# New prices for single operations in the planner of a hybrid decoder layer

## The chip, the cores and the metric

The kernel is one program on one core of a Trainium2 chip. Its time is device microseconds (us) of that core, from the program's start to its end; several runs are taken and the median is given. The engines are named as the profile names them: PE is the matrix engine TensorE (PEld its loads of weights), DVE is VectorE, ACT is ScalarE, POOL is GpSimd, SP is SyncE, which issues nearly all loads.

## The reference

One decoder layer for 512 tokens of width 2048, all in float32:

```python
mod_all = silu(c) @ w_ada + b_ada                    # 6 vectors of 2048
h = rms_norm(x, norm1_g) * (1 + sc1) + sh1
u = h @ w_in                                         # conv | q | 3 x (k, v) | gates
y_conv = B * causal_depthwise_conv3(C * H)
y_attn = g0 * compressed + g1 * selected + g2 * window   # 8 heads x 128, 2 kv heads
x = x + g1 * ([rms_norm(y_conv) | rms_norm(y_attn)] @ w_out)
h = rms_norm(x, norm2_g) * (1 + sc2) + sh2
x = x + g2 * (relu(h @ w_ff1) ** 2 @ w_ff2)          # inner width 8192
out = rms_norm(x, normf_g)
```

## The kernel before

**How the work is tiled.** Tokens lie along the free dimension, 512 of them or two halves of 256; the 2048 channels are 16 blocks of 128 partitions. Every large product is made of three matmuls, high x high, high x low and low x high: each operand is split into a high part (a copy on ACT into the type fp32r) and a low part (a subtraction on DVE, `x - high`). So a block of weights of 128 x 1024 (512 KB) comes by a load of SP, costs ACT one copy and DVE one subtraction, and feeds 24 matmuls of TensorE. The two large products of the feed-forward part are made by seven block products instead of eight (B1, U6, T5, B2, T7, B3, T4 in the code, by sums of the four blocks of weights on DVE and of the tokens); the results of some of the seven are combined out of PSUM on DVE, and the chains "a", "b" and "c" (table `CHAIN`) say which of the seven add onto one PSUM bank. T4 adds onto the bank of T7 after T7's sum has been read from it.

**What runs in which order.** Three programs follow each other, each with a planner of its own:

1. The opening, the modulation vectors, the projections and the convolution (line 369, 16 passes). `mod_all` is made on DVE: 190 *dots* (`dot`, line 470) multiply 1024 weights by silu(c) on each of 128 partitions and sum them into one column; each takes a load of 512 KB into one of eight tiles wa. Meanwhile TensorE works through the key, value, convolution, gate and query columns. `rope` (line 659) rotates keys and queries with two *half rotations*, products on 64 partitions each.
2. Attention (line 1066, 6 passes), eight blocks of 128 queries and one kv head: scores s, a maximum, Exp on ACT, `cf = gate / sum` on DVE (a reciprocal and a product on 128 x 4), transposes on TensorE into pt, a split of these into tt (ACT, then DVE), and products pv. Between them stand the columns of `out_conv`, 16 blocks of 24 matmuls with weights from mix.
3. The rest of the output projection, the feed-forward part and the last norm (line 1233, one pass). The first product's results, squared, are split into gt (three tiles in turn, line 1259) and gb (one tile, line 1260) by `outcome` (line 1444) and stored to device memory g by GpSimd, 256 KB at a time; the second product loads them back. Weights of this part are split into a ring of three tiles hl (line 1240) and, for the first of the plan, tiles sg and gt.

**The planner.** Class `Order` stands between the code and the engines. `record` keeps each operation as a node with what it must follow: data, a tile's earlier readers, and the slots of the one ring of 29 tiles "m". `price` (line 126) gives each node a cost, the time for which it holds its engine, and a lag, after which another engine may use its result; on one engine, DVE or TensorE, the next operation may follow as soon as the cost is over. `plan` simulates the engines: it computes for each node the latest time at which it may begin (`late`, from the times at which TensorE wants its matmuls) and then takes, again and again, the node that can begin first, and among those the one with the earliest `late`. A load or store ends some time after a model of the wire (lines 308 and 309): 1.5 us from its issue at the least, its size at 340 GB/s (410 in the first 40 us), and 0.7 us (2.8 in the first 40 us). Stores into g count 1.3 times their size. With several passes the matmuls' planned times of one pass are the wanted times of the next, and in every second the planned order of the matmuls is kept; the pass with the shortest total wins (line 223). With one pass the matmuls stay in the order of the code, apart from a few marked as floating, among them those that sum squares and spread a norm's factor over the partitions.

`emit` (line 212) then issues all operations sorted by their planned begin (line 237). Each engine takes its own in that order, whatever happens: an operation that waits holds back all that stand behind it on its engine. The planned times themselves reach the chip in no other way.

Of the kernel before, what the change touches and what calls it, by code (L numbers as in the profile page):

```python
# [16 lines left out]
P = 128  # L17
# [40 lines left out]
class Order:  # L58
# [67 lines left out]
    def price(self, eng, op, out, ins, kw):  # L126

        n = Order.width(out)
        if "dma" in op:
            return (0.42 if eng == "sync" else 0.55), 0.0  # L130
        if eng == "tensor":
            if op == "matmul" and ins[0].name.startswith("ones"):
                return n * 0.0017, 0.2
            if op == "matmul" and ins[0].dtype == F32:
                return max(self.wide[0], n * self.wide[1]) * out.shape[0] / P, 0.2
            return (0.109 if op == "transpose" else max(0.1, n * self.pace)), 0.2
        if eng == "scalar":
            aps = len(ins) - 1
            more = 0.1 if kw.get("accum_out") is not None else 0.0
            return (0.18 if n < 16 else 0.09 + 0.00084 * n + (0.09 * max(0, aps) if not more else 0.19)), 0.16  # L140
        if eng == "gpsimd":
            return 0.15 + 0.0024 * n, 0.3
        if op == "tensor_reduce":
            rows = max(Order.width(x) for x in ins)
            return 0.18 + 0.00104 * rows * (1.75 if n > 16 else 1), 0.14
        if n < 16:
            return (0.2 if op == "reciprocal" else 0.14), 0.14
        if op == "scalar_tensor_tensor":
            return 0.14 + 0.00101 * n + (0.087 if kw.get("accum_out") is not None else 0.0), 0.14
        if op in ("tensor_scalar", "tensor_copy", "memset") and all(  # L150
                x.space != bass.MemoryType.PSUM for x in [out] + ins):
            return 0.13 + 0.0005 * n, 0.14
        strided = any(abs(list(x.ap)[-1][0]) > 1 for x in [out] + ins)
        return 0.068 + n * (0.00185 if strided else 0.00104) + (0.1 if out.shape[0] < P else 0.0), 0.14

    def record(self, eng, op, real, args, kw):
        is_ap = lambda x: hasattr(x, "dep_tracking_offset")
# [90 lines left out]
    def plan(self, ideal, t, fixed):  # L248
        nodes = self.nodes
        ends = {}  # L250
        for name, by in self.seen.items():
            for i in set(by):
                ends.setdefault(i, []).append(name)
        users = {name: len(set(v)) for name, v in self.seen.items()}
        mine = sorted((n for x in nodes for n in x.born), key=lambda n: int(n.rsplit("_", 1)[1]))
        rank = {n: k for k, n in enumerate(mine)}

        for x in reversed(nodes):
            move = x.cost + x.lag if not x.size else 2.5 + x.size / Order.RATE
            x.late = min([nodes[s].late - (move if nodes[s].eng != x.eng or x.eng not in ("tensor", "vector") else x.cost)  # L260
                          for s in x.succs] + [ideal.get(x.i, t + 10.0 - x.due)])

        free = dict.fromkeys(("tensor", "vector", "scalar", "sync", "gpsimd"), 0.0)
        wire = 0.0
        ready = {e: [] for e in free}
        lanes = {}
        for i in fixed or [x.i for x in nodes if x.eng == "tensor" and not x.loose]:
            lanes.setdefault(0 if fixed else nodes[i].lane, []).append(i)
        for lane in lanes.values():
            lane.reverse()  # L270
        slots = sorted([0.0] * (self.count - len(self.outer)))
        given = []
        while slots and len(given) < len(mine):
            given.append(slots.pop(0))
        for x in nodes:
            x.left, x.ready = len(x.preds), 0.0
            if not x.left and (x.eng != "tensor" or x.loose):
                ready[x.eng].append(x)
        out = []
        while len(out) < len(nodes):  # L280
            best = None
            for e in free:
                c = [(x, 0, None) for x in ready[e]]
                if e == "tensor":
                    c = [(x, -1, None) for x in ready[e]]
                    c += [(nodes[q[-1]], k, q) for k, q in lanes.items() if q and not nodes[q[-1]].left]
                for x, k, q in c:
                    at = max(free[e], x.ready + x.slack, wire - 2.0 if x.size else 0.0)
                    if x.born:
                        last = max(rank[n] for n in x.born)  # L290
                        if last >= len(given):
                            continue
                        at = max(at, given[last])
                    key = (at, k, x.late, x.i)
                    if best is None or key < best[0]:
                        best = key, x, q
            (at, *_), x, q = best
            e = x.eng
            if q is not None:
                q.pop()  # L300
            else:
                ready[e].remove(x)
            x.begin = at
            free[e] = at + x.cost
            end = at + x.cost + x.lag
            if x.size:
                wire = max(wire, at + 1.5)
                wire += x.size / (Order.RUSH if wire < self.rush else Order.RATE)
                end = wire + (2.8 if wire < self.rush else 0.7)
            for n in ends.get(x.i, ()):  # L310
                users[n] -= 1
                if not users[n] and (n in rank or n in self.outer) and n not in self.kept:
                    if len(given) < len(mine):
                        given.append(max([end] + given[-1:]))
            for s in x.succs:
                y = nodes[s]
                y.left -= 1
                y.ready = max(y.ready, free[e] if e == y.eng and e in ("tensor", "vector") else end)
                if not y.left and (y.eng != "tensor" or y.loose):
                    ready[y.eng].append(y)  # L320
            out.append(x)
        return max(free.values()), out
# [1497 lines left out]
```

## Time and profile before

| what | us |
|---|---|
| median of 3 runs | 2052.33 |
| lowest and highest | 2050.72 and 2052.61 |
| the profiled execution | 2051.98 |
| its span, first to last instruction | 2050.2 |
| granted TensorE clock over the span | 0.998 of full speed |

The profile is of one execution. What lies around its span (1.78 us) is the start and end of the program. Busy times overlap between engines, and TensorE's busy time is a model of pipelined matmuls, so it is to be read together with the number of matmuls in a stretch. The profile's lines all name line 162, since `record` issues everything; instructions are told apart by their tiles: "pf<-tk,hl" writes tile pf and reads tk and hl. An idle time stands in brackets with what ended it.

### The profile page before, as it was taken

The numbers are of one execution on the slowest core, as the hardware profiler recorded it, in microseconds if no ns is written. First come the engines' busy times: TensorE is split into PE (matmuls) and PEld (weight loads), VectorE is DVE, ScalarE is ACT, GpSimd is POOL, SyncE is SP. The second block draws the span as 40 slices with busy tenths as digits, with TensorE's granted clock in tenths as the row PEclk, the third lists the DMA queues.
The fourth block names the chain that finished last, engine by engine and source line by source line (L and its number), as shares of the span: only waits on it lengthen the run. The fifth ranks groups of instructions, "written<-read, shape, count | busy, mean of one in ns | idle before, by whom it ended". The sixth has DMA issues, their size and how long they took to land. (4 is left out here: it accounts for less than half of the span.)

```text
span 2050.2 us, 38160 instructions
## 1 busy us (share of the span) xinstructions
PE 2039.0 (99%) x15038; PEld 1905.5 (93%) x15038; DVE 1854.6 (90%) x3007; ACT 1031.0 (50%) x1564; POOL 128.2 (6%) x244
## 2 busy tenths in 40 slices
PE   9999999999999999999999999999999999999998
PEld 7888778898888789999999999999999999999998
DVE  8999768898898657999999999999999999999998
ACT  7664222323556436766666666666433333333355
POOL 0000000000000001122121121211000000000000
PEclk9999999999999999999999999999999999999999
DMA  9996789997221253567767767679876466466452
GB/s 388 341 344 215 285 311 342 339 334 256 77 97 34 92 205 116 179 211 216 216 197 212 210 201 215 202 207 333 301 272 240 144 242 240 145 234 243 152 171 104
DMA packets 142676, 454.25 MB, mean 222 GB/s; under 512 B 15776, under 2 KB 18208, under 8 KB 142496
## 3 DMA queue, kind: packets, MB, share of 16 engines
q1 hardware_dynamic: 108448, 387.83, 54.7%
q0 software_dynamic: 34048, 63.98, 10.3%
q8 instruction: 118, 1.93, 0.4%
q14 instruction: 62, 0.51, 0.1%
HBM read 383.59 MB, written 68.16 MB: 220 GB/s over the span
## 5 line engine op out<-in xcount | busy, mean ns | idle before, releaser
L162 PE MATMUL pf<-tk,hl 128*128 128x256 f32 x10704 | 1218.9, 276 | 2.3 <-ACT hl L162 1.1
L162 PEld LDWEIGHTS pf<-tk,hl 128*128 128x128 f32 x10704 | 1217.2, 188 | 2.8 <-ACT hl L162 1.3
L162 ACT ACTIVATE hl<-rw 128x1024 fp32r<-128x1024 f32 x269 | 285.6, 1062 | 323.7 <-PE pf L162 276.1
L162 DVE TENSOR_TENSOR hl<-rw,hl 128x1024 fp32r<-128x1024 f32 (+2 forms) x351 | 335.9, 967 | 28.6 <-ACT hl L162 27.7
L162 ACT ACTIVATE hl<-sg 128x1024 fp32r<-128x1024 f32 x180 | 191.0, 1062 | 230.6 <-PE pf L162 186.1
L162 DVE SCALAR_TENSOR_TENSOR t<-wa,cs 128x1024 bf16<-128x1024 f32 x190 | 232.0, 1221 | 28.5 <-DMA wa<-in_w_ada 25.2
L162 PE MATMUL ps<-h_m,wh 128*128 128x512 f32 x1080 | 248.8, 389 | 0.0
L162 PEld LDWEIGHTS ps<-h_m,wh 128*128 128x128 f32 x1080 | 202.5, 188 | 43.1 <-issue 1.2
L162 ACT ACTIVATE wh<-raw 128x1024 fp32r<-128x1024 f32 (+1 forms) x105 | 112.0, 1067 | 248.1 <-PE ps L162 207.5
L162 DVE TENSOR_TENSOR hl<-sg,hl 128x1024 fp32r<-128x1024 f32 (+2 forms) x193 | 187.8, 984 | 23.9 <-ACT hl L162 23.8
L162 PE MATMUL ps<-h,wh 128*128 128x512 f32 x840 | 195.8, 390 | 0.7 <-DVE h L162 0.5
L162 PEld LDWEIGHTS ps<-h,wh 128*128 128x128 f32 x840 | 157.0, 188 | 35.4 <-issue 1.2
L162 DVE TENSOR_TENSOR wh<-raw,wh 128x1024 fp32r<-128x1024 f32 (+1 forms) x106 | 129.9, 1225 | 27.3 <-ACT wh L162 26.7
L162 DVE TENSOR_TENSOR sg<-sg,rw 128x1024 f32<-128x1024 f32 x120 | 146.7, 1222 | 3.0
L162 DVE SCALAR_TENSOR_TENSOR x<-pf,mod,x 128x256 f32<-128x256 f32 (+1 forms) x280 | 128.8, 484 | 13.7 <-PE pf L162 12.2
L162 POOL DMA_DIRECT2D g<-gt x192 | 101.2, 532 | 382.1 <-DVE gt L162 217.9
L162 PE MATMUL pw<-mix,wh 128*128 128x512 f32 x384 | 108.6, 404 | 0.0
L162 ACT ACTIVATE t<-t 128x512 f32<-128x512 f32 (+2 forms) x130 | 74.0, 572 | 11.8 <-DVE t L162 9.9
L162 PEld LDWEIGHTS pw<-mix,wh 128*128 128x128 f32 x384 | 68.5, 189 | 10.6
L162 DVE TENSOR_TENSOR sg<-rw 128x1024 f32<-128x1024 f32 x60 | 73.0, 1217 | 5.7 <-DMA rw<-in_w_f 5.5
L162 DVE TENSOR_TENSOR rw<-rw 128x1024 f32<-128x1024 f32 x60 | 72.9, 1215 | 0.0
L162 DVE TENSOR_TENSOR gt<-t,gt 128x512 fp32r<-128x512 f32 x96 | 65.5, 683 | 0.5 <-ACT gt L162 0.5
(222 smaller groups left out, 1708.8 us busy)
## 6 DMA issues: line engine op xcount, KB each, us to landing
rw<-in_w_f SPq DMA_DIRECT2D x263, 512.0 KB, 4.2
wa<-in_w_ada SPq DMA_DIRECT2D x192, 512.0 KB, 6.4
tk<-g SPq DMA_DIRECT2D x114, 512.0 KB, 6.5
g<-gt POOLq DMA_DIRECT2D x192, 256.0 KB, 5.0
raw<-in_w_conv SPq DMA_DIRECT2D x32, 512.0 KB, 4.6
x<-in_xt SPq DMA_DIRECT2D x16, 512.0 KB, 5.5
raw<-in_w_kv SPq DMA_DIRECT2D x16, 512.0 KB, 5.1
raw<-in_w_cv SPq DMA_DIRECT2D x16, 512.0 KB, 4.5
```

Of the source, the lines that this page charges most:

```text
L162: x.i, x.eng, x.call = len(self.nodes), eng, (lambda: real(*args, **kw))
```

## The change

Prices of single operations in `price`, and the planned end of a store by GpSimd in `plan`. No operation is added or removed, and none changes its operands; the planner is run with the new prices.

```diff
         if eng == "scalar":
-            aps = len(ins) - 1
-            more = 0.1 if kw.get("accum_out") is not None else 0.0
-            return (0.18 if n < 16 else 0.09 + 0.00084 * n + (0.09 * max(0, aps) if not more else 0.19)), 0.16
+            if n < 16:
+                return 0.09 * len(ins), 0.16
+            base = (0.045 if ins[0].space == bass.MemoryType.PSUM else 0.09) + 0.00084 * n
+            return base + (0.09 * (len(ins) - 1) if kw.get("accum_out") is None else 0.19), 0.16
...
         if op == "tensor_reduce":
             rows = max(Order.width(x) for x in ins)
-            return 0.18 + 0.00104 * rows * (1.75 if n > 16 else 1), 0.14
+            return 0.06 + 0.00104 * rows * (1.75 if n > 16 else 1), 0.14
         if n < 16:
-            return (0.2 if op == "reciprocal" else 0.14), 0.14
+            return (0.09 if op == "reciprocal" else 0.14 if op == "scalar_tensor_tensor" else 0.075), 0.14
         if op == "scalar_tensor_tensor":
-            return 0.14 + 0.00101 * n + (0.087 if kw.get("accum_out") is not None else 0.0), 0.14
+            given = hasattr(kw["scalar"], "dep_tracking_offset")
+            return (0.14 + 0.00101 * n if given else 0.08 + 0.00103 * n), 0.14
+        if op == "memset":
+            return 0.01 + 0.00075 * n, 0.14
+        if op == "tensor_scalar" and ins[0].space == bass.MemoryType.PSUM:
+            return 0.135 + 0.00104 * n, 0.14
...
         strided = any(abs(list(x.ap)[-1][0]) > 1 for x in [out] + ins)
-        return 0.068 + n * (0.00185 if strided else 0.00104) + (0.1 if out.shape[0] < P else 0.0), 0.14
+        return 0.068 + n * (0.0017 if strided else 0.00104), 0.14
...
                 wire += x.size / (Order.RUSH if wire < self.rush else Order.RATE)
-                end = wire + (2.8 if wire < self.rush else 0.7)
+                end = wire + (2.8 if wire < self.rush else 2.3 if e == "gpsimd" else 0.7)
```

`n` is the number of elements of the output on one partition, `ins` are the operands that lie in memory (so a scale or bias that is a column counts as one), and `given` is true where the scalar of the operation is a column of values, false where it is a number.

| operation | price before | price after |
|---|---|---|
| dot, 1024 | 1.261 | 1.135 |
| half rotation, 512 | 0.700 | 0.600 |
| ACT copy out of PSUM, 512 | 0.520 | 0.475 |
| reciprocal on 128 x 4 | 0.200 | 0.090 |
| product on 128 x 4 | 0.140 | 0.075 |
| a store of 256 KB into g, issue to end | 3.2 | 4.8 |

## The prediction

> **What bounds the kernel now.** I read the page first, then the busy time by stage, then who makes TensorE wait, then the timeline at those waits. The page:
>
> ```profile
> span 2050.2 us, 38160 instructions
> ## 1 busy us (share of the span) xinstructions
> PE 2039.0 (99%) x15038; PEld 1905.5 (93%) x15038; DVE 1854.6 (90%) x3007; ACT 1031.0 (50%) x1564; POOL 128.2 (6%) x244
> ```
>
> The reader is to see that TensorE has 11.2 us of idle time in all (2050.2 - 2039.0), and that VectorE is the next fullest engine. The busy time by stage follows; the columns are the stretch, its length, then busy time and (instructions) of PE, PEld, DVE, ACT and POOL, the granted clock, DMA share and GB/s:
>
> ```profile
> 25.00:200.00 175.00, 174.52 (x770) 144.12 (x769) 168.76 (x252) 105.62 (x192) 0.00 (x0) 1.00 0.85 320
> 200.00:500.00 300.00, 300.00 (x1570) 251.71 (x1569) 249.50 (x383) 81.52 (x109) 0.00 (x0) 1.00 0.88 318
> 500.00:700.00 200.00, 200.00 (x1040) 162.99 (x1039) 164.92 (x455) 112.89 (x269) 0.00 (x0) 1.00 0.24 80
> 700.00:775.00 75.00, 75.00 (x417) 65.67 (x416) 42.60 (x56) 28.77 (x40) 3.65 (x6) 1.00 0.46 157
> 775.00:950.00 175.00, 173.37 (x1507) 173.03 (x1506) 164.04 (x303) 120.88 (x209) 26.28 (x48) 1.00 0.59 181
> 950.00:1400.00 450.00, 450.00 (x3969) 450.00 (x3968) 428.91 (x592) 286.01 (x402) 87.94 (x167) 1.00 0.69 208
> 1400.00:1990.00 590.00, 590.00 (x5197) 590.00 (x5196) 567.85 (x847) 245.86 (x257) 10.15 (x20) 1.00 0.66 229
> 1990.00:2050.00 60.00, 52.80 (x460) 52.07 (x459) 51.16 (x101) 34.69 (x70) 0.00 (x0) 0.97 0.28 97
> ```
>
> A busy TensorE could still hide slow matmuls, so I divide: 450.00 us by 3969 is 113.4 ns a matmul, and 590.00 by 5197 is 113.5. Two long stages at one pace, at a granted clock of 1.00, mean that nothing holds TensorE there. Idle time stands in three rows only: 0.48 us in the first, 1.63 in the fifth (175.00 - 173.37), 7.20 in the last, nearly all of that behind the last matmul. Who makes TensorE wait (total, times, longest):
>
> ```profile
> PE pf L162 <- ACT hl L162: 1.1, 1, 1.1
> PE ps L360 <- DVE eps L363: 1.1, 1, 1.1
> PE pf L162 <- DVE hl L162: 0.6, 1, 0.6
> PE pf L162 <- DVE t L162: 0.5, 1, 0.5
> PE ps L162 <- DVE h L162: 0.5, 1, 0.5
> PE ps L162 <- DVE sq L162: 0.4, 2, 0.2
> PE pf L162 <- DVE rs L162: 0.4, 1, 0.4
> ```
>
> Without the second and sixth, which lie in the opening before the dense work, that is 3.1 us of stalls in 2050. The change adds and removes no instruction; it gives other prices to a planner, so it can only alter the order in which each engine takes the same instructions. **What an order can win is those 3.1 us, a little of the opening, and small bubbles priced below; what it can lose has no such ceiling.**
>
> **The change, part by part.**
>
> *1. GpSimd's stores count longer.* A planned store ends 1.5 us after its issue, plus 256 KB x 1.3 at 340 GB/s = 1.0 us, plus 0.7: 3.2 us. With 2.3 in place of 0.7 it is 4.8. Both fifth-stage stalls lead here:
>
> ```profile
> 922.26 0.41 DVE L162 TENSOR_TENSOR t<-pf,t 128x256 f32<-128x256 f32 x1
> ...
> 922.82 19.32 PE L162 MATMUL pf<-tk,hl 128*128 128x256 f32 x168 [0.51 <-DVE t L162]
> ...
> 942.70 0.42 DVE L162 TENSOR_TENSOR t<-pf,t 128x256 f32<-128x256 f32 x1
> ...
> 943.26 2.00 PE L162 MATMUL pf<-tk,hl 128*128 128x256 f32 x15 [1.12 <-ACT hl L162]
> ```
>
> TensorE resumes both times 0.15 us after VectorE's subtraction t<-pf,t ends (922.67, 943.12). So I read the second as the same wait although the view names ACT: product T4 adds onto the bank from which product T7 has yet to be read (`sub(y[:, 0], b, y[:, 0])`). VectorE was late with it, and some 12 to 15 us earlier ScalarE, which VectorE follows for every low half, had stood still on a store:
>
> ```profile
> 910.43 0.42 ACT L162 ACTIVATE gb<-t 128x256 fp32r<-128x256 f32 x1 [1.04 <-DMA g<-gb]
> ```
> ```profile
> 928.08 0.42 ACT L162 ACTIVATE gb<-t 128x256 fp32r<-128x256 f32 x1 [1.06 <-DMA g<-gb]
> ```
> ```profile
> 923.31 0.53 POOL L162 DMA_DIRECT2D g<-gb  x1 [9.86 <-DVE gb L162]
> ```
> ```profile
> g<-gt POOLq DMA_DIRECT2D x192, 256.0 KB, 5.0
> ```
>
> The store issued at 923.31 freed its tile at 928.08, 4.77 us later; the 192 others take 5.0 in the median. 4.8 is therefore right and 3.2 was 1.6 short. The Trainium skill's page "DMA: Bandwidth & Descriptors" ("Anatomy of one DMA", SWDGE path) fits 2.0 us plus bytes at 436 GB/s, an estimate of 2.6 us here, by which the old price was ample; the two rows above disagree with it. With the later date the plan can put another operation ahead of gb on ScalarE, and order the subtraction ahead of gt's and gb's low halves on VectorE. I take the whole 1.63: **-1.6 us**, bounds -1.6 and 0. If the cover goes, the next thing late is the ring of three hl tiles. POOL's queue itself has room (87.94 us busy in 450).
>
> *2. Dots.* 190 of them fall from 0.14 + 1.034 + 0.087 = 1.261 to 0.08 + 1.055 = 1.135, 23.9 us less planned VectorE time. None runs faster. Two cases on VectorE:
>
> ```profile
> 30.50 1.23 DVE L162 SCALAR_TENSOR_TENSOR t<-wa,cs 128x1024 bf16<-128x1024 f32 x1
> 31.65 0.08 DVE L162 DVE_READ_ACCUMULATOR t<-wa,cs 128x1 f32 x1
> 31.77 1.23 DVE L162 SCALAR_TENSOR_TENSOR t<-wa,cs 128x1024 bf16<-128x1024 f32 x1
> ```
> ```profile
> 36.63 1.22 DVE L162 SCALAR_TENSOR_TENSOR t<-wa,cs 128x1024 bf16<-128x1024 f32 x1
> 37.79 0.08 DVE L162 DVE_READ_ACCUMULATOR t<-wa,cs 128x1 f32 x1
> 37.79 0.68 DVE L162 TENSOR_TENSOR h<-t,h 128x512 fp32r<-128x512 f32 x1
> ```
>
> A dot before another dot holds VectorE 1.27 us from start to start (31.77 - 30.50), a dot before something else 1.16. The old price fits the first, the new one the second, 0.13 short for the first. In the first stage the order on TensorE is that of the steps and the dots stand in order of due time; a common shift of their prices hardly reorders them. I take **0**. Bounds: a gain up to the stage's 0.48 us, a loss as in the rival "late".
>
> *3. Small operations, half rotations, reduces.* A reciprocal falls from 0.20 to 0.09, the small product from 0.14 to 0.075. In attention they stand as a chain:
>
> ```profile
> 545.94 0.17 DVE L162 RECIPROCAL cf<-sm 128x4 f32<-128x4 f32 x1
> 546.14 0.17 DVE L162 TENSOR_TENSOR cf<-cf,gates 128x4 f32<-128x4 f32 x1
> 546.35 0.35 DVE L162 TENSOR_SCALAR p<-p,cf 128x256 f32<-128x256 f32 x1
> ```
>
> Start to start they take 0.20 and 0.21: the new prices are 0.11 and 0.135 short where each waits for the one before. With 24 such pairs (3 branches x 8 blocks) the plan promises 24 x 0.245 = 5.9 us too much over 200 us in which VectorE has 35 us idle (200 - 164.92) and TensorE 16 column blocks of out_conv to fill with. That cover hides it: **0**; without it, up to +5.9. Half rotations (0.70 to 0.60) and reduces go in the same direction. The other prices (memsets, strided sums, a product with a number as its scalar 1.174 to 1.135, four scalings out of PSUM 0.067 dearer) move a few dozen operations by less than 0.1 us each, all beside a full TensorE: 0, and with that cover gone no more than the loss above.
>
> The Trainium skill, "VectorE: DVE Perf Modes", section "The DRAIN you can't avoid", says that the next operation doesn't start until the pipeline is empty, wait or no wait; that speaks against these cuts. The chain above agrees; the rows at 37.79, where two instructions start together 0.06 us before the dot of 1.22 has ended, do not.
>
> *4. Copies out of PSUM.* ScalarE's price falls by 0.045. The transposed tiles of attention are just in time already:
>
> ```profile
> PEld pv L162 <- ACT tt L162: 7.1, 32, 0.3
> ```
>
> Planned need between transposes and the next product was 0.52 + 0.16 + 0.20 = 0.88 us, now 0.835. Fillers of 512 columns are priced 512 x 0.000456 = 0.233: four (0.93) covered it, three (0.70) still do not. So **0**, bound 32 x 0.045 = +1.4, and as much the other way if the bubbles pack better.
>
> *5. The ends.* The opening waits for x and runs one chain; the prices on it fall by 0.11 + 2 x 0.126 = 0.36 us, so 0 within 0.4 either way. At the end a broadcast waits 0.4 us for the reciprocal rs (last row of the waits); promised 0.11 earlier, it may be placed earlier and wait longer: **+0.1**. The output's store follows the last matmul as before.
>
> **Sum:** -1.6 + 0.1 = -1.5 us. The profiled execution took 2051.98 us (1.78 around its span), so 2050.5; the median of the runs shown is 0.35 above it: 2050.8. About 0.2%, 4.1 us, is what a measurement of this kernel tells from no change, so I forecast no change that can be told.
>
> **Rivals.**
>
> *Late (slower).* One mechanism: the new prices are those of an operation with an independent one behind it, and VectorE runs behind the plan where it has no idle time. Place: 25 to 200 us, 6.24 us idle of 175, and the fullest part of attention. Taking 70 dots there, half of them in pairs, 35 x 0.13 = 4.6 us are promised and not delivered; a quarter of attention's 5.9 adds 1.5. It decides once low halves come later than the step that TensorE has in hand, about 5.6 us of work by the planner's own step. For it: 96% busy there, and old prices that held 0.1 us to spare per dot. Against: TensorE met one stall of 0.5 us in that stage, and an unchanged order isn't made late by its price. 2052.3 + 4.6 + 1.5 = 2058.4 at full size, half of it inside "no change".
>
> *Stores are not the cause.* Only hl's ring or VectorE's load keeps T4 waiting; ScalarE has nothing else to do in those 1.06 us. Then part 1 gives nothing: 2052.4.
>
> *Packs better.* The dots' margin was what spaced the plan; all 3.1 us of stalls and half of 32 bubbles of some 0.09 (estimated: 0.3 us waits of PEld with the one in flight hiding 0.2) go, 3.1 + 1.4 = 4.5: 2047.8.
>
> *Reshuffled.* The orders change and the same stalls turn up elsewhere: 2051 to 2054.
>
> **Chances.** Forecast (both stalls of part 1 gone) 0.38; stores not the cause 0.20; reshuffled 0.20; late 0.16, of which 0.14 beyond 4.1 us; packs better 0.06. So faster by over 0.2%: 0.07; within: 0.79; slower: 0.14. The range takes in "packs better" and most of "late": 2047.0 to 2057.0.
>
> **What would show it.** Part 1: after the change, ScalarE's waits for DMA g<-gb and TensorE's two stalls of the fifth stage are gone, and that row has 175 us busy. Parts 2 and 3: the stage rows keep their TensorE busy time; a TensorE wait on DVE h, h_m or wh in 25 to 200, or on DVE tt or nm in attention, over 0.3 us would show "late". Part 4: the count of 32 stays within a few. The forecast is wrong if 950 to 1990 shows idle TensorE time or a pace above 114 ns.

## The result and the profile after

The changed kernel takes 2062.15 us (median of 4 runs, 2061.38 to 2064.24) against 2051.52 for the kernel before on the same chip: ratio 1.0054, 95% interval 1.004 to 1.0068. It is slower by about 11 us; the forecast was 2050.8, with a range up to 2057.0. Its profiled execution has a span of 2059.6 us, 9.4 more than before's.

The page of the changed kernel, the lines that answer to those shown of before:

```profile
span 2059.6 us, 38158 instructions
## 1 busy us (share of the span) xinstructions
PE 2045.6 (99%) x15038; PEld 1902.9 (92%) x15038; DVE 1854.3 (90%) x3007; ACT 1033.3 (50%) x1564; POOL 128.2 (6%) x244
```

The work is the same (VectorE's busy time differs by 0.3 us); only time in which nothing useful runs has been added. The stretches of before, read in the changed kernel (stretch, length, then busy time and instructions of PE, PEld, DVE, ACT, POOL, granted clock, DMA share, GB/s):

```profile
25.00:200.00 175.00, 174.15 (x767) 143.37 (x766) 167.31 (x251) 104.55 (x188) 0.00 (x0) 1.00 0.85 320
200.00:500.00 300.00, 298.86 (x1560) 249.90 (x1559) 251.33 (x388) 83.11 (x112) 0.00 (x0) 1.00 0.88 317
500.00:700.00 200.00, 198.79 (x1008) 155.84 (x1006) 159.38 (x443) 109.37 (x260) 0.00 (x0) 1.00 0.21 72
700.00:775.00 75.00, 75.00 (x381) 63.64 (x380) 43.21 (x55) 31.10 (x43) 2.26 (x4) 1.00 0.50 175
775.00:950.00 175.00, 174.12 (x1507) 173.95 (x1507) 159.01 (x296) 116.03 (x203) 25.92 (x47) 1.00 0.56 172
950.00:1400.00 450.00, 450.00 (x3967) 450.00 (x3967) 428.25 (x594) 288.80 (x406) 88.29 (x168) 1.00 0.68 208
```

The third row carries most of the loss, and PE's busy time hardly shows it: 198.79 of 200 is still 99%, but only 1008 matmuls fall into the stretch instead of 1040. PEld's busy time does show it, 155.84 us instead of 162.99. Short waits of TensorE stay hidden because the ends of matmuls are modelled: a stall that the timeline of before puts at 0.51 us (at 922.82) is 0.68 from start to start, and the one of 1.12 is 1.28. The second row lost ten matmuls (1560 instead of 1570). The last row has the old pace, 450.00 / 3967 = 113.4 ns.

Stages are therefore best measured from start to start. The rows of the tiles give the first and last start of each kind of matmul (the two times after the durations); before first, then after:

```profile
L162 PE MATMUL pw<-mix,wh x384: 387/395/486, 529.3 to 710.4; 128*128 128x512 f32 x192
L162 PE MATMUL pf<-mixa,wh x48: 389/389/395, 710.6 to 721.3; 128*128 128x512 f32 x48
L162 PE MATMUL ps<-h,wh x840: 387/389/504, 24.7 to 528.1; 128*128 128x512 f32 x168
```
```profile
L168 PE MATMUL pw<-mix,wh x384: 387/395/486, 532.0 to 720.0; 128*128 128x512 f32 x192
L168 PE MATMUL pf<-mixa,wh x48: 389/389/389, 720.2 to 730.9; 128*128 128x512 f32 x48
L168 PE MATMUL ps<-h,wh x840: 387/389/504, 24.4 to 530.8; 128*128 128x512 f32 x168
```

From here on "opening" is the start of the first ps<-h,wh, "projections" the time from there to the first pw, "attention" from the first pw to the first pf, "feed-forward" from there to the last matmul's start. The same starts, read from each trace to more digits (the differences are taken before rounding):

| us | opening | projections | attention | feed-forward | tail |
|---|---|---|---|---|---|
| before | 24.7 | 504.6 | 181.3 | 1332.9 | 6.7 |
| after | 24.4 | 507.6 | 188.2 | 1332.6 | 6.7 |
| difference | -0.3 | +3.0 | +6.9 | -0.3 | +0.1 |

Attention lost 6.9 us and the projections 3.0; they make the whole. Who made TensorE wait in the changed kernel (five of its rows, the longest behind the opening):

```profile
PE pv L168 <- DVE tt L168: 1.0, 3, 0.4
PE pf L168 <- DVE t L168: 0.9, 1, 0.9
PE ps L168 <- DVE vv L168: 0.8, 1, 0.8
PE pf L168 <- DVE hl L168: 0.7, 1, 0.7
PE ps L168 <- DVE h L168: 0.6, 1, 0.6
```

Two of them are new, DVE tt in attention and DVE vv in the projections; two smaller new ones in the projections, for wh and t, are 0.3 us each. To see all that was lost, each matmul's time to the next start can be set against the median of its shape: of attention's 6.9 us, 4.4 lie directly ahead of the products pv, which read tt, and 0.9 ahead of the scores s. Of the projections' 3.0, 1.9 lie at the waits for wh, t and vv; the rest isn't traced. One of the three waits for tt, in the timeline (VectorE's rows and the matmul; others left out):

```profile
543.33 0.69 DVE L168 TENSOR_TENSOR rt<-qr,rot 64x512 f32<-64x512 f32 x1
...
544.04 0.18 DVE L168 RECIPROCAL cf<-sm 128x4 f32<-128x4 f32 x1
...
544.25 0.17 DVE L168 TENSOR_TENSOR cf<-cf,gates 128x4 f32<-128x4 f32 x1
...
544.46 0.35 DVE L168 TENSOR_SCALAR p<-p,cf 128x256 f32<-128x256 f32 x1
544.73 0.68 DVE L168 TENSOR_TENSOR tt<-pt,tt 128x512 fp32r<-128x512 f32 x1
...
545.47 0.50 PE L168 MATMUL pv<-tt,vv 128*128 128x512 f32 x1 [0.41 <-DVE tt L168]
```

From the half rotation to the scaling VectorE takes 544.46 - 543.33 = 1.13 us. The new prices allow 0.600 + 0.090 + 0.075 = 0.765, the old ones 0.700 + 0.200 + 0.140 = 1.040. The plan is 0.37 us short over three operations, and TensorE, whose product stands behind the two fillers that the plan gave it, waits 0.41 for the low half of tt. Two of the three steps are a chain, the reciprocal, its product and the scaling that reads it. The first is not: the reciprocal doesn't read the rotated half, and still it starts 0.71 us after it. In this trace a half rotation takes 0.61 us ahead of some others of its kind and 0.70 to 0.72 ahead of nearly everything else, dependent or not. Waits like this one are mostly smaller, and show on the loads of weights (before, then after):

```profile
PEld pv L162 <- ACT tt L162: 7.1, 32, 0.3
PEld pv L162 <- DVE tt L162: 3.4, 17, 0.3
PEld s L162 <- DVE nm L162: 0.5, 3, 0.2
```
```profile
PEld pv L168 <- DVE tt L168: 9.2, 29, 0.8
PEld pv L168 <- ACT tt L168: 6.6, 29, 0.4
PEld s L168 <- DVE nm L168: 2.1, 8, 0.4
```

ScalarE's half of tt is waited for as before; VectorE's half is late 29 times instead of 17, and the maxima nm, which it makes too, 8 times instead of 3.

Where VectorE had idle time to make up for this is seen in before, in the first 80 us of attention and in the rest of it (columns as above):

```profile
530.00:610.00 80.00, 80.00 (x440) 66.13 (x439) 77.09 (x244) 48.03 (x131) 0.00 (x0) 1.00 0.22 73
610.00:710.00 100.00, 100.00 (x508) 80.13 (x508) 76.69 (x186) 57.41 (x128) 0.00 (x0) 1.00 0.20 69
```

VectorE is idle for 2.9 us of the first 80 and for 23.3 of the next 100. In the changed kernel 16 of the 29 waits are over 0.23 us; 11 of these lie in its first 80 us of attention, and ahead of 14 of the 16 VectorE had no idle time in the two microseconds before the late operation.

The new wait in the projections:

```profile
418.38 1.22 DVE L168 SCALAR_TENSOR_TENSOR t<-wa,cs 128x1024 bf16<-128x1024 f32 x1
419.52 0.08 DVE L168 DVE_READ_ACCUMULATOR t<-wa,cs 128x1 f32 x1
419.52 0.75 DVE L168 SCALAR_TENSOR_TENSOR y<-y,vec,sacc 128x512 f32<-128x512 f32 x1
420.19 1.08 DVE L168 TENSOR_TENSOR vv<-ps,vv 128x256 fp32r<-128x256 f32 x3
```

Here a dot and a product of the convolution group, neither of which this matmul reads, stand ahead of the low halves of vv; TensorE waits for these 0.8 us, until 420.66.

### The profile page after: what moved, and what is told of

Its sections match the earlier page's. It is cut to its first block, busy times and chain, and to the rows that moved or that the text cites. A ratio compares the mean times of both kernels' runs of the same rounds, so it can differ in the third digit from the quotient of the medians.

```text
span 2059.6 us, 38158 instructions
## 1 busy us (share of the span) xinstructions
PE 2045.6 (99%) x15038; PEld 1902.9 (92%) x15038; DVE 1854.3 (90%) x3007; ACT 1033.3 (50%) x1564; POOL 128.2 (6%) x244
## 5 line engine op out<-in xcount | busy, mean ns | idle before, releaser
L168 DVE TENSOR_TENSOR hl<-sg,hl 128x1024 fp32r<-128x1024 f32 (+2 forms) x193 | 188.4, 987 | 24.9 <-ACT hl L168 24.7
```

The source lines that it names most:

```text
L168: x.i, x.eng, x.call = len(self.nodes), eng, (lambda: real(*args, **kw))
```

## The experiments

**Theory "late".** The new prices are right for an operation with an independent one behind it and short for a chain in which each waits for the one before; where the plan has chains it promises VectorE time that isn't there, and TensorE waits. **Rivals:** ScalarE's cheaper copies out of PSUM took fillers away ("copies"); or any change of prices throws a plan about, whichever way it goes ("reshuffled").

The three planners work one by one, so each kernel tests three things, one for each stage. All are the changed kernel with three more arguments to a planner: `new`, the groups of prices that have their new values (all the others have the old ones); `drain`, a gap that an operation of VectorE must keep from an earlier one of VectorE on which it depends; `dve`, a factor on VectorE's costs. The default is the changed kernel.

```diff
+ALL = frozenset(("small", "reduce", "half", "copy", "dot", "memset", "strided", "scaled", "store"))
...
-    def __init__(self, tc, tag, count, passes=1, pace=0.000456, rush=0.0):
+    def __init__(self, tc, tag, count, passes=1, pace=0.000456, rush=0.0, new=ALL, drain=0.0, dve=1.0):
+        self.new, self.drain, self.dve = set(new), drain, dve
...
-        x.cost += self.extra
+        x.cost = x.cost * (self.dve if eng == "vector" else 1.0) + self.extra
...
-                y.ready = max(y.ready, free[e] if e == y.eng and e in ("tensor", "vector") else end)
+                wet = self.drain if e == "vector" else 0.0
+                y.ready = max(y.ready, free[e] + wet if e == y.eng and e in ("tensor", "vector") else end)
```

"small" are operations under 16 elements, on VectorE and ScalarE; "dot" is every product with two operands and a scalar; "copy" ScalarE's reads of PSUM; "store" the later end of GpSimd's stores. What was measured, from the profiled execution of each kernel (they ran on more than one chip), all in one table (P, A and F are the arguments for projections, attention and feed-forward; "old" is `new=()`):

| kernel | P | us | A | us | F | us |
|---|---|---|---|---|---|---|
| before | old | 504.6 | old | 181.3 | old | 1332.9 |
| after | all new | 507.6 | all new | 188.2 | all new | 1332.6 |
| e1_attention_new | old | 504.9 | all new | 188.5 | old | 1332.8 |
| e2_small_old | all but dot | 509.9 | all but small, reduce | 182.2 | store | 1330.9 |
| e3_half_old | dot | 510.6 | all but half | 187.4 | all but store | 1333.6 |
| e4_drain | all, drain | 505.7 | all, drain | 182.3 | all, drain | 1329.0 |
| e5_small_alone | dot, drain | 504.5 | small | 184.6 | store, drain | 1329.1 |
| e6_reduce_alone | half | 505.2 | reduce | 182.7 | old, drain | 1334.9 |
| e7_cheap | old x 0.955 | 513.3 | old x 0.955 | 184.9 | old x 0.955 | 1339.7 |
| e8_dear | old x 1.045 | 505.3 | old x 1.045 | 181.0 | old x 1.045 | 1342.4 |
| e9_best | dot, drain | 506.2 | old | 181.3 | all, drain | 1329.0 |
| e10_copy_alone | copy | 505.9 | copy | 181.7 | all but dot | 1331.8 |
| e11_small_first | small | 505.4 | half | 182.2 | all but copy | 1331.6 |
| e12_small_reduce | all but dot, drain | 504.4 | small, reduce | 186.7 | store | 1331.3 |

Where the same plan ran in two profiles, attention differs by up to 0.3 us (181.3 and 181.3; 188.2 and 188.5), feed-forward by up to 0.4 (1330.9 and 1331.3), the projections by up to 1.7 (504.5 and 506.2). So in the last, differences under 2 us say little.

**One stage alone (e1_attention_new).**

```diff
-    nc = order = Order(..., passes=16, pace=0.000444, rush=40.0)
+    nc = order = Order(..., passes=16, pace=0.000444, rush=40.0, new=())
...
-    nc = order = Order(tc, x1[0].tensor.tag, NMAIN, pace=0.000444)
+    nc = order = Order(tc, x1[0].tensor.tag, NMAIN, pace=0.000444, new=())
```

> The new prices in attention's planner alone; the two other planners have the old ones. In the profiles of before and after, attention (first matmul on pw to first matmul on pf) takes 181.3 and 188.3 us, what lies ahead of it 529.3 and 532.0, what follows to the last matmul 1332.9 and 1332.6. If the three plans act one by one: attention 188 (within 0.5), ahead of it 529.3, behind it 1332.9, the whole about 7 us over before, ratio 1.0034. If the loss comes from what one stage leaves to the next: attention under 186.

Measured: 188.5 in attention and the values of before in the other two; the whole 2058.67 us against 2052.38, ratio 1.0031 (1.002 to 1.0041). The plans act one by one, and two thirds of the loss are attention's own. The two other stages have the orders of before on TensorE and VectorE, operation by operation; in attention 258 of VectorE's 371 operations stand at another place than before.

**Which price in attention.** The small operations and reduces get their old prices, then the half rotations:

```diff
-    nc = order = Order(tc, mix[0].tensor.tag, NMAIN, passes=6)
+    nc = order = Order(tc, mix[0].tensor.tag, NMAIN, passes=6, new=ALL - {"small", "reduce"})
```

> Attention: all new prices but those of operations under 16 elements and of reduces, which keep the old. Theory late (the new prices of small operations that wait for each other promise VectorE time that it does not have): attention back to 181.3 to 183. Rival copies (ScalarE's cheaper copies out of PSUM take fillers from between the transposes and the products): attention stays at 186 to 189. Rival reshuffled (any other set of prices throws the order about): anything from 181 to 189. Opening and projections: all new prices but those of dots. Theory late for the dots: 529 to 530; otherwise it stays at 532. Feed-forward: the old prices with the store's new one alone. Theory of the prediction: the two stalls near 922 and 942 us both go, 1331.2; if the store is not their cause, 1332.9.

> Attention: all new prices but those of half rotations, which keep the old. Theory late with the small operations: 186 to 188, since 8 half rotations at 0.1 us are at most 0.8 of the 6.9 us. If the half rotations alone are the cause: 182. Opening and projections: the old prices with the dots' new one alone. Theory late for the dots: 531 to 532 of 529.3; if dots are not the cause: 529.3. Feed-forward: all new prices but the store's. If the store's price is what took one of the two stalls away: both are back, 1332.9; else 1332.6.

With the old prices for small operations and reduces alone attention is back at 182.2; "copies" is out, since the cheaper copies are still in that plan. Without the half rotations' new price it stays at 187.4. Feed-forward with all prices but the store's takes 1333.6, and both stalls of before are back (TensorE waits 1.2 us for ACT hl and 0.5 for ACT t); with the store's price alone it wins 2.0 us; TensorE's waits there are now only the two at the end:

```profile
PE pf L177 <- DVE hl L177: 0.7, 1, 0.7
PE pf L177 <- DVE rs L177: 0.4, 1, 0.4
```

In the projections both expectations were missed, and the result went against a simple reading: the dots' price alone costs 6.0 us, but all the others without it cost 5.3, and all together only 3.0. With the dots' price alone TensorE waits for VectorE:

```profile
PE ps L177 <- DVE vv L177: 2.2, 2, 1.9
PE ps L177 <- DVE t L177: 1.0, 2, 0.6
PE ps L177 <- DVE wh L177: 0.7, 1, 0.7
```

In all three plans the longest of these waits is the one for vv.

**The gap (e4_drain).** All new prices stay, and the plan learns of chains:

```diff
-    nc = order = Order(tc, mix[0].tensor.tag, NMAIN, passes=6)
+    nc = order = Order(tc, mix[0].tensor.tag, NMAIN, passes=6, drain=0.115)
```

and the same for the two others.

> All new prices in all three planners, and one more rule in the plan: on VectorE an operation that depends on an earlier one of VectorE may begin 0.115 us after that one's cost is over, not at once. Theory late: the plan is true again for chains (reciprocal and product, dot behind dot, half rotation and sum), attention 181 to 182.5, ahead of it 529 to 530, the whole within 2 us of before (ratio 0.999 to 1.001). Rival copies: attention stays at 186 to 189. Rival reshuffled: attention anywhere from 181 to 189.

Attention 182.3, projections 505.7, the whole 2050.93 us, ratio 0.9992 (0.9983 to 1.0002). What lies ahead of attention takes 531.0 instead of the expected 529 to 530; the rest came as "late" has it. One rule takes back 6.0 of attention's 6.9 us and 1.9 of the projections' 3.0 while every new price stays; the whole is level with before because feed-forward won 3.9. The 0.9 that stay in attention are as much as the half rotations' price costs by itself (below), and a gap between dependent operations doesn't mend a half rotation ahead of an independent one; that they are the same 0.9 is not shown. VectorE's order is as far from before's as in the changed kernel (259 of 371 operations in attention at another place, against 258), which speaks against "reshuffled". A kernel with the same time added to all of VectorE's operations in place of the gap was not run. How the gap works is to be seen on VectorE, at the same place in attention as above:

```profile
545.07 0.18 DVE L177 RECIPROCAL cf<-sm 128x4 f32<-128x4 f32 x1
545.16 0.67 DVE L177 TENSOR_TENSOR t<-rt 128x512 f32<-128x512 f32 x1
545.74 0.16 DVE L177 TENSOR_TENSOR cf<-cf,gates 128x4 f32<-128x4 f32 x1
545.81 1.08 DVE L177 TENSOR_REDUCE t<-t 128x128 f32<-128x512 f32 x1
```

The reciprocal holds VectorE 0.09 us here (545.16 - 545.07), the new price to the digit, with an independent operation behind it; the product holds it 0.07. Its product stood right behind 18 of the 24 reciprocals before and behind 23 in the changed kernel, mostly 0.20 to 0.21 us from start to start; in this kernel it stands behind 7. Of the 17 others, 16 hold VectorE for 0.08 to 0.10 us. Feed-forward came out 3.9 us shorter than before, which no theory had asked for. None of before's four stalls is left in it; from start to start they had cost 0.68, 1.28, 0.80 and 0.52 us, 3.3 of the 3.9. TensorE has no idle time at its beginning:

```profile
775.00:950.00 175.00, 175.00 (x1527) 175.00 (x1526) 163.60 (x305) 121.25 (x210) 27.49 (x50) 1.00 0.60 184
```

**Parts alone (e5_small_alone, e6_reduce_alone, e12_small_reduce).**

```diff
-    nc = order = Order(tc, mix[0].tensor.tag, NMAIN, passes=6)
+    nc = order = Order(tc, mix[0].tensor.tag, NMAIN, passes=6, new=("small",))
```

and `("reduce",)`, and `("small", "reduce")`; the other stages as in the table.

> Attention: the old prices, with the new ones for operations under 16 elements alone. Theory late (chains of small operations): 185 to 187, against 181.3 with all old and 188.3 with all new, since they promise 24 x 0.245 = 5.9 us of the 7.8 that small operations and reduces together promise. If only the set as a whole does harm: 181 to 183. From the first dense matmul to the first on pw: the old prices, the dots' new one, and 0.115 us between dependent operations of VectorE. Theory late: 505 (504.6 before, 510.6 with the dots' new price and no such gap). If the dots' price is wrong apart from that: 508 to 511. Feed-forward: the store's new price and the same gap: 1329 if these two make the gain of the run with all prices and the gap (1329.0), 1331 if the gap adds nothing to the store's price (1330.9).

> Attention: the old prices with the reduces' new one alone. Theory late: 182 to 184 (16 reduces on 128 x 128 at 0.12 us, 1.9 us promised). If the reduces are the cause and not the small operations: 186 to 188. First dense matmul to first on pw: the old prices with the half rotations' new one alone; 12 of them at 0.1 us promise 1.2 us: 504.6 to 505.8; if any new price throws that stage: over 507. Feed-forward: the old prices with the gap of 0.115 us between dependent operations of VectorE: 1331 if gap and store's price add up (2.0 and 1.9 us), 1329 if the gap alone does it, 1332.9 if it needs the store's price.

> Attention: the old prices and the new ones of operations under 16 elements and of reduces, both and nothing else. Theory late: 187 to 189, the whole loss of the new prices (188.3), since alone they gave 184.6 and 182.7 and all the others together 182.2. If it needs other prices as well: 184 to 186. First dense matmul to first on pw: all new prices but the dots', with the gap of 0.115 us. If what threw that stage without the dots' price (509.9) is again operations that wait for each other: 504.5 to 506.5; otherwise 508 to 511. Feed-forward: the old prices and the store's new one, the same plan as in the run with the small operations' old prices: 1330.9 within 0.5 if that gain belongs to the plan and not to the run.

Attention: 3.3 us for the small operations, 1.4 for the reduces, 5.4 for both, of 6.9; the half rotations alone add 0.9 (below), and taking them out of the full set gave back 0.8. The expectation for the small operations alone, 185 to 187, was missed by 0.4 us, and that for both together, 187 to 189, by 0.3: the half rotations belong to it. The projections with the dots' price and the gap are back at 504.5 (506.2 in a second kernel), and with all prices but the dots' and the gap at 504.4. With the dots' price and the gap TensorE's wait for vv is 0.3 us instead of 2.2. Feed-forward shows that gap and store's price need each other: 1330.9 with the store's price, 1334.9 with the gap alone (2.0 worse than before), 1329.1 with both. The expected sum, 1331, didn't come; with the gap alone ScalarE waits for GpSimd's stores 7 times, 12.1 us, against 5 times and 5.1 before:

```profile
ACT gt L177 <- DMA g<-gt: 7.0, 4, 2.6
...
ACT gb L177 <- DMA g<-gb: 5.1, 3, 1.8
```

**Spread evenly, both ways (e7_cheap, e8_dear).**

```diff
-    nc = order = Order(tc, mix[0].tensor.tag, NMAIN, passes=6)
+    nc = order = Order(tc, mix[0].tensor.tag, NMAIN, passes=6, new=(), dve=0.955)
```

and 1.045, in all three stages.

> The old prices, all of VectorE's costs times 0.955: in attention, with 165 us of VectorE, 7.4 us promised away, about what the new prices of small operations and reduces promise (7.8), but spread evenly. Theory late as a matter of load: attention 185 to 189, projections over 508, feed-forward over 1335. Theory late as a matter of the chains alone: attention 182 to 184. Rival reshuffled: each stage anywhere from its value before to 7 us over it, and no less with the opposite change in the next run.

> The old prices, all of VectorE's costs times 1.045: the opposite of the run before, as far from the old prices. Theory late: attention 181 to 183, from the first dense matmul to the first on pw 504 to 506, feed-forward 1329 to 1333: dear prices cost nothing as long as the plan still finds work for TensorE. Rival reshuffled: as bad as the cheap ones. A plan that gets too loose (TensorE's order filled late): attention over 184 with few stalls of over 0.1 us.

In attention and the projections this speaks against "reshuffled": the cheap plan loses 3.6 and 8.7 us, the dear one -0.3 and 0.7, at the same distance from the old prices. Attention's 184.9 lies between the two ranges that were expected of "late", for load and for chains alone: 7.4 us promised evenly cost 3.6, and the 7.8 promised in small operations and reduces cost 5.4. Too much VectorE time in the plan does harm in either form, and more where the chains are. In feed-forward both lose, 6.8 and 9.5; the dear plan was expected at 1329 to 1333, and there "late" does not hold by itself. In the dear plan ScalarE waits for stores ten times, up to 3.6 us:

```profile
ACT gb L177 <- DMA g<-gb: 15.6, 10, 3.6
```

That would follow if dear VectorE work pushes the low halves, and with them the stores, behind what the plan of the stores allows; it was not tried with the store's new price, so it stays an argument.

**The rest (e10_copy_alone, e11_small_first).**

```diff
-    nc = order = Order(tc, mix[0].tensor.tag, NMAIN, passes=6)
+    nc = order = Order(tc, mix[0].tensor.tag, NMAIN, passes=6, new=("copy",))
```

and `("half",)`; in the projections `("copy",)` and `("small",)`.

> The old prices and the copies out of PSUM's new one alone, in projections and attention. Theory late through chains on VectorE: no harm, 504.6 to 506 and 181.3 to 182.5. Rival copies: attention 184 or more, through products that wait for ScalarE's tt. If cheap copies are what throws the projections without the dots' price (509.9): 507 to 510. Feed-forward: all new prices but those of products with a number as their scalar: 1331 if these are what kept one stall alive with all new prices (1332.6; the store's price alone 1330.9), otherwise 1332 to 1333.

> Projections: the old prices and the new ones of operations under 16 elements alone. If they are what throws that stage without the dots' price (509.9): 507 to 510; theory late would allow only little here, since few such operations wait for each other there: 504.6 to 506. Attention: the old prices with the half rotations' new one alone: 181.3 to 182.5 (0.8 us promised). Feed-forward: all new prices but the copies out of PSUM: 1331 if those kept the one stall alive, otherwise 1332 to 1333.

Copies alone cost attention 0.4 us. Of the four groups tried alone in the projections only the dots throw the stage (the others: 505.2 to 505.9), though all prices without the dots' cost 5.3. Since the gap takes that away as well, chains are probably in it; which of them isn't settled. In feed-forward the stall of 0.9 us that stayed in the changed kernel needs both groups: it falls to 0.2 without the price of the products with two operands and a scalar, and is gone without that of the copies. Both plans take about 1 us less than the whole set.

**A version that beats both (e9_best).**

```diff
-    nc = order = Order(..., passes=16, pace=0.000444, rush=40.0)
+    nc = order = Order(..., passes=16, pace=0.000444, rush=40.0, new=("dot",), drain=0.115)
...
-    nc = order = Order(tc, mix[0].tensor.tag, NMAIN, passes=6)
+    nc = order = Order(tc, mix[0].tensor.tag, NMAIN, passes=6, new=())
...
-    nc = order = Order(tc, x1[0].tensor.tag, NMAIN, pace=0.000444)
+    nc = order = Order(tc, x1[0].tensor.tag, NMAIN, pace=0.000444, drain=0.115)
```

> The parts that did best, put together: projections with the old prices, the dots' new one and the gap of 0.115 us (504.5); attention with the old prices (181.3); feed-forward with all new prices and the gap (1329.0). If the three plans act one by one, with an opening of 24.7 and a tail of 6.6 us: a span of 2046.2, 4.0 less than before; ratio 0.998, its interval below 1.

2050.2 us against 2052.49, ratio 0.9989 (0.998 to 0.9998): faster than before by about 2 us, half of what was expected. Its attention and feed-forward came as expected; its profiled execution had an opening of 27.9 us and projections of 506.2, so its span (2051.1) says less than the comparison of runs.

## Why the prediction was wrong

- **What bounds the kernel** was right: TensorE, with little to win by any order, and no ceiling on what an order can lose. The best kernel found wins about 2 us, the worst lost some 20. The 3.1 us were a little too low as a ceiling, since each stall costs some 0.16 us more from start to start than the wait that the view shows; feed-forward alone won 3.8 to 3.9 in three kernels.
- **Step 1, the stores**, was right in mechanism and size for that price by itself. Forecast -1.6; the store's price alone gave -2.0 and -1.6. ScalarE's wait for g<-gb is gone after the change, and the wait for g<-gt fell from 3.0 to 0.3 us. Within the full set only 0.3 of it showed, since one of the two stalls on T4 stayed: TensorE resumes at 932.90, 0.15 us after the subtraction t<-pf,t has ended (932.33 + 0.42), the wait that the prediction read out of before's two stalls. So the sign that both would be gone didn't come. "4.8 is therefore right" says too much: stores into g took from 2.3 to over 9 us in before. The 192 from gt have a median of 5.0, but the 32 from gb one of 2.6, which is the estimate that the prediction set aside; only the first five of these, where the stalls were, took 3.0 to 5.1.
- **Step 2, the dots**, failed. The prediction said that a common shift of their prices hardly reorders them: 0. It cost 6.0 us alone, and with the gap between dependent operations nothing (504.5) or at most 1.6 (506.2). What came late were operations on VectorE that TensorE wanted: with the dots' price alone it waits 2.2 us for vv, 1.0 for t and 0.7 for wh, and with the gap 0.3 for vv. That the dots were placed ahead of these because they were priced short is the reading of one place (at 418.38).
- **Step 3, the small operations**, is the step that failed most. Its arithmetic was right: two prices 0.11 and 0.135 short, 24 times, 5.9 us promised too much, and with 16 reduces at 0.12, 1.9 us, it is 7.8; with the new prices of these two groups alone attention lost 5.4. What failed was the sentence "That cover hides it: 0", and it is the step by which the forecast missed: 6.9 us in attention in place of nothing. VectorE's idle time lies elsewhere than the lateness, 2.9 us of it in the first 80 of attention, where 11 of the 16 longer waits are, and ahead of 14 of the 16 there was none. TensorE's fillers stand in a fixed order that was planned with the short prices. A sum over a stage hid nothing.
- **Step 4, the copies**, held: +0.4 us alone, within its bounds of 0 and 1.4 and hardly more than two profiles of one plan differ, and 29 waits for ScalarE's tt in the changed kernel against 32.
- **Step 5, the ends**, can't be told: the opening differs by up to 2.6 us between two kernels with one plan. The wait for rs, which was to grow by 0.1 us, went from 0.4 to 0.3.
- **The rival "late"** named the mechanism and the signs to look for, and was given 0.16. Of its two places it had one right: it put 4.6 us into 25 to 200 us and a quarter of 5.9 into attention. Into 25 to 200 us only three matmuls fewer fall (767 instead of 770), into 200 to 500 ten fewer, and attention lost 6.9 us. The argument against it, that an unchanged order isn't made late by its price, was beside the point, since the order did change. Its 2058.4 was too low, and the range ended lower still, at 2057.0.
- **The rule on the empty pipeline** that the prediction took from the Trainium skill, "VectorE: DVE Perf Modes", section "The DRAIN you can't avoid", is only half of what stands there: the section goes on, "A next op that is not held starts earlier". The traces have both cases: 0.20 to 0.21 us from the reciprocal to its product, mostly 0.09 to an independent operation, for an operation of 0.18. So the section doesn't speak against the new prices as such. A plan that knows only one of the two cases is wrong somewhere; a price and a gap state both.

## What to carry to other kernels

A price taken from a trace carries the neighbour it was measured with: the start-to-start time of a small instruction differs by a factor of two with what stands behind it, so cost and dependency gap have to be two numbers. Where the bounding engine has hardly any idle time, cheaper prices for the others can win little and can spend the margin that kept them on time. Cover for a late operation is counted at its own place in its engine's order, from the operations that stand ahead of it, and not from the stage's idle time.

## What the runs showed of the hardware

One instruction on VectorE can have several times: a reciprocal on 128 x 4 lasts 0.18 us in the profile, holds the engine 0.08 to 0.10 us ahead of an independent operation (16 of 17 cases in e4_drain) and mostly 0.20 to 0.21 ahead of its own product. Dependence isn't all that counts: a product on 64 partitions takes 0.71 us ahead of the reciprocal at 544.04, which doesn't read it, and 0.61 ahead of some others of its kind. Why is not shown.

The opening, up to the first dense matmul, took between 22.8 and 27.9 us over the fourteen profiles. Kernels whose first plan is the same had 24.7 and 23.1 us (before and e1_attention_new), 25.3 and 27.9 (e5_small_alone and e9_best). Of the stages it differs most between two kernels with one plan, and by more than the 1.5 us that were forecast as the gain.
